# A decoder trunk in split fp32: the tiles of the split weights made 256 bytes longer, and consecutive chunks begun at eight different offsets

## The chip, the cores and the metric

The kernel runs on one core of one Trainium2 chip. The metric is device time in microseconds of one execution; lower is better. The kernel before took 2110.1 us, the median of 3 runs (2109.5 to 2110.94).

## The reference

The reference is a decoder trunk of two layers on 256 positions of width 2048, all in float32. Layer A mixes with a gated MLP over chunks of 128 positions, layer B with 12 heads of latent attention; both attend to 256 memory tokens with 4 heads, and both end in a feed-forward block of width 5632 with a causal convolution of width 3. Cut to the products that fill the time:

```python
def conv_ffn(h, w_up, cw, cb, w_down):
    a = h @ w_up                                   # 2048 x 11264
    ap = jnp.pad(a, ((0, 0), (CONV_W - 1, 0), (0, 0)))
    c = sum(ap[:, k:k + S] * cw[k] for k in range(CONV_W)) + cb
    gate, val = c[..., :D_FF], c[..., D_FF:]
    return (jax.nn.silu(gate) * val) @ w_down      # 5632 x 2048

for l in range(DEPTH):
    h = rmsnorm(x, g_mix[l])
    ...                                            # z = h @ w_in, main mixer, memory attention
    x = x + jnp.concatenate([main, mo], axis=-1) @ w_out[l]
    x = x + conv_ffn(rmsnorm(x, g_ffn[l]), w_ffn_up[l], conv_w[l], conv_b[l], w_ffn_down[l])
return rmsnorm(x, g_final)
```

## The kernel before

Every large product is computed in three matmuls of the type fp32r. Each operand is split into a high part (rounded to fp32r) and a low part (the rest): x = hi + lo, w = whi + wlo, and the product is hi whi + hi wlo + lo whi. The activations stand transposed and split in one tile (xhl, mainhl, h, memhl, qhl, chl): for each of the blocks of 128 features 512 columns, 256 of hi and 256 of lo.

**A chunk** (method `chunk`, L92 to L129) is 128 x 1024 numbers of a weight matrix, as a rule two blocks of 128 rows by 512 columns. SP issues its DMA into a tile raw (L101). ACT rounds it into whi (L121, or L126 where a gain is multiplied in, L117 for the queries' weights), DVE takes the difference raw - whi into wlo (L122, L127, L118). There are four buffers each of raw, whi and wlo, 4096 bytes per partition each.

**Two kinds of products** use a chunk:

- `gemm_fm` (from L163, with `mm_fm` from L139): the weights are the loaded operand of TensorE, in blocks of 128 x 128, the activations stream. L144 streams 512 columns (hi and lo) under whi, L148 streams the 256 columns of hi under wlo and adds them to the half of the result that belongs to lo. Chunks are taken in pairs: 32 matmuls of L144 and 32 of L148, and the order of the two turns from pair to pair.
- `gemm_tm` (with `mm_tm`, L196 to L201): the activations are loaded, the weights stream, 512 columns: L199 (hi, whi), L200 (hi, wlo), L201 (lo, whi).

Every matmul carries its own weight load. Results are evicted by ACT and DVE (`join`, L239 and L241; `split`, L246 and L247), with POOL beside them.

**The order.** Each engine's order of instructions is laid down when the program is built: a scheduler with a timeline moves instructions past each other where data and buffers allow it. How many buffers a tile has therefore enters the order. SP's queue holds the weights' DMAs in the order of the chunks; a DMA waits for DVE to have read the buffer's earlier contents.

**What else the change touches.** `conv_consts` (from L337) loads four small matrices craw by DMA (L344), transposes each on TensorE (L345) into one PSUM tile and copies that to cT; it runs once for each layer, near the end of the memory's products (90 to 101 us). Their space is given to layer A's tiles later, among them positions (L356, L358). `rope_angles` (L353 to L386) makes cos and sin, `rope_tables` (L395) transposes them. The tile u (L741 to L745) is used in layer A's gate after that. In layer B's attention `scores` (from L878) makes a head's products (L885 to L887), and ACT writes their exponentials into a tile p (L896), DVE scales it (L901); `turn` transposes p on TensorE (L908), ACT copies that to pT (L910), and `attend` multiplies (L917, L918). The loop works on the heads in pairs, some steps apart. L624 and L625, in the feed-forward block's convolution, work on a tile from its second and third element on.

The few lines that say how a chunk is used:

```python
hi = self.wp.tile([P, 1024], F32R, tag="whi", name=self.uid("whi"), bufs=4)
lo = self.wp.tile([P, 1024], F32R, tag="wlo", name=self.uid("wlo"), bufs=4)
...
nc.scalar.activation(hi[:, :n], raw[:, :n], AF.Copy)
nc.vector.tensor_tensor(lo[:, :n], raw[:, :n], hi[:, :n].bitcast(F32), ALU.subtract)
...
mm(acc[:, :], wh, x, start=first, stop=last)                  # L144
mm(acc[:, S:], wl, x[:, :S], start=False, stop=False)         # L148
```

Of the kernel before, what the change touches and what calls it, by code (L numbers as in the profile page):

```python
# [8 lines left out]
F32 = mybir.dt.float32  # L9
F32R = mybir.dt.float32r  # L10
# [6 lines left out]
P = 128  # L17
D = 2048
S = 256
# [10 lines left out]
HALF = ROPE // 2  # L30
THETA = 10000.0
EPS = 1e-6
FF_GROUPS = (4, 4, 3)


def exact_pieces(value, bits, count):
# [33 lines left out]
class Kernel:  # L70
    def __init__(self, ctx, tc, t, out):
        self.tc, self.nc, self.t, self.out = tc, tc.nc, t, out
        self.ctx = ctx
        self.n = 0
        pool = lambda name, bufs=1, **k: ctx.enter_context(tc.tile_pool(name=name, bufs=bufs, **k))
        self.cp = pool("cp")
        self.wp = pool("wp")
        self.ap = pool("ap")
        self.ps = pool("ps", 8, space=bass.MemoryType.PSUM)
# [12 lines left out]
    def chunk(self, src, nk, ncol, gains=None, twice=False, heads=None, raw=None):  # L92
        nc, n = self.nc, nk * ncol
        loaded = raw is not None
        if not loaded:
            raw = self.wp.tile([P, 1024], F32, tag="raw", name=self.uid("raw"), bufs=4)
        hi = self.wp.tile([P, 1024], F32R, tag="whi", name=self.uid("whi"), bufs=4)
        lo = self.wp.tile([P, 1024], F32R, tag="wlo", name=self.uid("wlo"), bufs=4)
        view = lambda x: x[:, :n].rearrange("p (k c) -> p k c", k=nk)
        if not loaded:  # L100
            nc.sync.dma_start(out=view(raw), in_=src)  # L101
        if twice:

            full = self.wp.tile([P, 1024], F32, tag="raw", name=self.uid("raw"), bufs=4)
            both = lambda x: x.rearrange("p (k o c) -> p k o c", o=2, c=ncol)
            src4 = raw[:, :n].rearrange("p (k o c) -> p k o c", k=nk, o=1).to_broadcast([P, nk, 2, ncol])
            g4 = gains.rearrange("p (k a b) -> p k a b", a=1, b=1).to_broadcast([P, nk, 2, ncol])
            nc.vector.tensor_tensor(both(full), src4, g4, ALU.mult)
            nc.scalar.activation(hi, full, AF.Copy)
            nc.vector.tensor_tensor(lo, full, hi.bitcast(F32), ALU.subtract)  # L110
            return tuple(x.rearrange("p (k c) -> p k c", k=nk) for x in (hi, lo))
        if heads is not None:

            s = view(raw).rearrange("p k (h c) -> p k h c", h=2)
            for c0, c1 in ((0, heads), (heads, ncol // 2)):
                o = lambda x: view(x)[:, :, 2 * c0 : 2 * c1].rearrange("p k (h c) -> p k h c", h=2)
                nc.scalar.activation(o(hi), s[:, :, :, c0:c1], AF.Copy)  # L117
                nc.vector.tensor_tensor(o(lo), s[:, :, :, c0:c1], o(hi).bitcast(F32), ALU.subtract)  # L118
            return view(hi), view(lo)
        if gains is None:  # L120
            nc.scalar.activation(hi[:, :n], raw[:, :n], AF.Copy)  # L121
            nc.vector.tensor_tensor(lo[:, :n], raw[:, :n], hi[:, :n].bitcast(F32), ALU.subtract)  # L122
        else:
            for k in range(nk):
                s = slice(k * ncol, (k + 1) * ncol)
                nc.scalar.activation(hi[:, s], raw[:, s], AF.Copy, scale=gains[k])  # L126
                nc.vector.scalar_tensor_tensor(  # L127
                    lo[:, s], raw[:, s], gains[k], hi[:, s].bitcast(F32), ALU.mult, ALU.subtract
                )  # L129
        return view(hi), view(lo)  # L130
# [206 lines left out]
    def conv_consts(self, l):  # L337
        nc, t = self.nc, self.t
        nf = 2 * FB
        acc = self.psum()  # L340
        for j in range(4):
            cr = self.tmp(self.gp, [nf, P], "craw", 4)
            src = t["conv_w"][l, j] if j < 3 else t["conv_b"][l]
            nc.sync.dma_start(out=cr, in_=src.rearrange("(k p) -> k p", p=P))  # L344
            nc.tensor.transpose(acc[:, j * nf : (j + 1) * nf], cr, self.ident[:nf, :nf])  # L345
        nc.vector.tensor_copy(self.cT[:, l], acc[:, : 4 * nf].rearrange("p (j k) -> p j k", j=4))
# [6 lines left out]
    def rope_angles(self, rt):  # L353
        nc, t = self.nc, self.t
        pi = rt.tile([2, P], I32, name="pos_i")
        nc.sync.dma_start(out=pi, in_=t["positions"].rearrange("b (a p) -> (b a) p", p=P))  # L356
        pf = rt.tile([2, P], F32, name="pos_f")
        nc.vector.tensor_copy(pf, pi)  # L358
        acc = self.psum()
        nc.tensor.transpose(acc[:, 0:2], pf, self.ident[:2, :2])  # L360
        pos = rt.tile([P, 2], F32, name="pos")
        nc.vector.tensor_copy(pos, acc[:, 0:2])
        inv = rt.tile([P, HALF], F32, name="inv")
        for i, v in enumerate(INV_FREQ):
            nc.gpsimd.memset(inv[:, i : i + 1], v)
        ang = rt.tile([P, 2, HALF], F32, name="ang")
        for a in range(2):
            nc.vector.tensor_scalar(ang[:, a, :], inv, pos[:, a : a + 1], None, ALU.mult)
        k = rt.tile([P, 2, HALF], F32, name="turns")
        magic = 12582912.0  # L370
        for scale, pieces in ((4096.0, two_pi_pieces(4096, 7, 9)), (1.0, two_pi_pieces(1, 10, 5))):
            nc.vector.tensor_scalar(k, ang, 1.0 / (2 * math.pi * scale), magic, ALU.mult, ALU.add)
            nc.vector.tensor_scalar(k, k, magic, None, ALU.subtract)
            for p in pieces:
                nc.vector.scalar_tensor_tensor(ang, k, -p, ang, ALU.mult, ALU.add)
        nc.vector.tensor_scalar(ang, ang, 3.1415925, -3.1415925, ALU.min, ALU.max)
        cos = rt.tile([P, 2, 4, HALF], F32, name="cos")
        sin = rt.tile([P, 2, 4, HALF], F32, name="sin")
        nc.scalar.activation(sin[:, :, 1, :], ang, AF.Sin)
        nc.scalar.activation(k, ang, AF.Sin, scale=0.5)  # L380
        nc.vector.tensor_tensor(k, k, k, ALU.mult)
        for j in range(4):
            nc.vector.tensor_scalar(cos[:, :, j, :], k, -2.0, 1.0, ALU.mult, ALU.add)
            if j != 1:
                nc.vector.tensor_scalar(sin[:, :, j, :], sin[:, :, 1, :], 1.0 if j == 3 else -1.0, None, ALU.mult)
        self.rope = cos, sin  # L386
# [220 lines left out]
    def ffn(self, l, after=None, to_tokens=None, tokens=None):  # L607
# [5 lines left out]
        with self.tc.tile_pool(name=self.uid("ff"), bufs=1) as fp:  # L613
            g0 = 0
            for part, ng in enumerate(FF_GROUPS):
                h = self.ap.tile([P, NB, 512], F32R, tag="big", name=self.uid("h"))
# [144 lines left out]
    def layer_b(self):  # L761
# [9 lines left out]
        with tc.tile_pool(name="lb", bufs=1) as lb:  # L771
# [73 lines left out]
            lp = ctx.enter_context(tc.tile_pool(name="lp", bufs=1))  # L845
# [32 lines left out]
            def scores(h):  # L878
                pr, j = divmod(h, 2)
                sc = self.psum()  # L880
                for qb in range(2):
                    n = P * (qb + 1)
                    o = sc[:, qb * P : qb * P + n]
                    q = slice(qb * P, (qb + 1) * P)
                    mm(o, qn[pr][:, j, q], kn[pr][:, j, :n], start=True, stop=False)  # L885
                    mm(o[:, qb * P :], self.identb, self.maskb, start=False, stop=False)
                    mm(o, qr[pr][:, q], krz[:, j, :n], start=False, stop=True)  # L887
                mx = self.tmp(lp, [P, 2], "mx", 4)
                den = self.tmp(lp, [P, 2], "den", 4)
                p = self.tmp(lp, [P, 3 * P], "p", 3)  # L890
                part = (slice(0, P), slice(P, 3 * P))
                for qb in range(2):
                    nc.vector.tensor_reduce(mx[:, qb : qb + 1], sc[:, part[qb]], AX.X, ALU.max)
                nc.vector.tensor_scalar(mx, mx, -scale, None, ALU.mult)
                for qb in range(2):
                    nc.scalar.activation(  # L896
                        p[:, part[qb]], sc[:, part[qb]], AF.Exp, bias=mx[:, qb : qb + 1], scale=scale, accum_out=den[:, qb : qb + 1]
                    )
                nc.vector.reciprocal(den, den)
                for qb in range(2):  # L900
                    nc.vector.tensor_scalar(p[:, part[qb]], p[:, part[qb]], den[:, qb : qb + 1], None, ALU.mult)  # L901
                pa[h] = p
# [30 lines left out]
            for i in range(n):  # L933
# [19 lines left out]
                if 1 <= i <= MH:  # L953
                    mscores(i - 1)
            scores(2 * n - 2)
            scores(2 * n - 1)
            for h in (2 * n - 4, 2 * n - 3):
# [95 lines left out]
```

## Time and profile before

| what | value |
|---|---|
| median of 3 runs | 2110.1 us |
| profiled execution, its own time | 2109.19 us |
| its span, first to last instruction | 2107.5 us |
| mean granted TensorE clock | 0.998 |
| HBM read, over the span | 387.88 MB, 185 GB/s |
| DMA queue of the weights, share of 16 engines | 56.7% |

The span is what the views of the profile divide; the profiled execution's own time has 1.7 us around it. PE is TensorE's matmuls, PEld its weight loads, DVE the vector engine, ACT the scalar engine, POOL GpSimd, SP the engine that issues most DMAs. A group's line names the line of the kernel, the engine, the operation, out<-in by the program's tile names, the shape, the count, then busy time and the mean in ns of one, then the idle time before. The mean of a matmul includes its passage through the array, which overlaps with the next one; the time from one matmul to the next is read from the chain of work in order of time.

### The profile page before, as it was taken

The page shows a single profiled execution, that of the slowest core. Times are in us where ns is not written, and L with a number is a line of the kernel's source. Part 1 is how long each engine was busy: PE and PEld are TensorE (multiplying, and loading weights), DVE is VectorE, ACT ScalarE, POOL GpSimd, SP SyncE. Part 2 cuts the span into 40 slices and gives each one's busy share as a digit, 9 for nine tenths or more (in the row PEclk, how much of TensorE's full clock was granted, in tenths as well). Part 3 has the DMA queues.
Part 4 walks back from the last instruction along what each step waited for, and adds up shares of the span by engine and source line. Part 5 has one row for each costly group of instructions (what it writes and reads, how often), then busy time and mean ns, then how long its engine had stood idle before and what let it go on. Part 6 is the DMA issues. An engine that isn't in the chain of part 4 may idle for free.

```text
span 2107.5 us, 30979 instructions
## 1 busy us (share of the span) xinstructions
PE 2090.7 (99%) x11600; PEld 1829.0 (87%) x11600; DVE 1460.8 (69%) x2156; ACT 1142.3 (54%) x1743; POOL 396.3 (19%) x380
## 2 busy tenths in 40 slices
PE   8999999999999999999999999999999999999998
PEld 7888888888888888888888888888888888888886
DVE  6655767777756777567798775777774677756775
ACT  7754654555535655445555564456554565535554
POOL 0100123312101211012244211321210121201220
PEclk9999999999999999999999999999999999999999
DMA  8565555655555565555555534555555656555554
GB/s 275 191 201 172 161 192 188 190 188 192 190 191 189 181 199 189 191 187 189 184 192 168 183 101 156 190 188 178 187 198 192 189 182 199 192 196 187 184 190 150
DMA packets 207852, 392.01 MB, mean 186 GB/s; under 512 B 14350, under 2 KB 23380, under 8 KB 207572
## 3 DMA queue, kind: packets, MB, share of 16 engines
q1 hardware_dynamic: 207268, 388.98, 56.7%
q8 instruction: 91, 1.49, 0.3%
q10 hardware_dynamic: 432, 1.05, 0.1%
q14 instruction: 61, 0.50, 0.1%
HBM read 387.88 MB, written 2.10 MB: 185 GB/s over the span
## 4 chain that ended last, share of the span: by engine, by line
PE 98%; DVE 1%; ACT 0%; DMA 0%; issue 0%; SPq 0%; ACTq 0%; DVEq 0%
PE ps L144 51%; PE ps L148 27%; PE ps L199 6%; PE ps L201 6%; PE ps L200 6%; PE ps L887 0%; PE ps L885 0%; PE ps L410 0%; PE ps L533 0%; PE ps L568 0%; PE ps L917 0%; DMA mtok<-in_mem 0%; PE ps L714 0%; PE ps L557 0%; PE ps L989 0%; DMA raw<-in_w_in_a 0%
## 5 line engine op out<-in xcount | busy, mean ns | idle before, releaser
L122 DVE TENSOR_TENSOR wlo<-raw,whi 128x1024 fp32r<-128x1024 f32 x660 | 842.6, 1287 | 481.7 <-ACT whi L121 358.4
L121 ACT ACTIVATE whi<-raw 128x1024 fp32r<-128x1024 f32 x660 | 698.4, 1060 | 694.9 <-PE ps L144 509.2
L144 PE MATMUL ps<-xhl,whi 128*128 128x512 f32 x3280 | 768.5, 390 | 0.0
L144 PEld LDWEIGHTS ps<-xhl,whi 128*128 128x128 f32 x3280 | 608.7, 188 | 121.6
L620 POOL TENSOR_TENSOR a<-js,rbc 128x256 f32<-128x256 f32 x176 | 231.3, 1327 | 1101.8 <-DVE js L241 1005.9
L148 PEld LDWEIGHTS ps<-xhl,wlo 128*128 128x128 f32 x3280 | 408.8, 191 | 11.1 <-DVE wlo L127 1.9
L148 PE MATMUL ps<-xhl,wlo 128*128 128x256 f32 x3280 | 413.9, 283 | 1.9 <-DVE wlo L127 1.5
L144 PE MATMUL ps<-h,whi 128*128 128x512 f32 x704 | 164.8, 390 | 0.0
L623 ACT ACTIVATE c<-a,cT 128x256 f32<-128x256 f32 x176 | 105.5, 600 | 98.2 <-POOL a L620 96.8
L144 PEld LDWEIGHTS ps<-h,whi 128*128 128x128 f32 x704 | 130.6, 188 | 26.0
L200 PE MATMUL ps<-wlo,h 128*128 128x512 f32 x352 | 136.8, 389 | 0.0
L199 PE MATMUL ps<-whi,h 128*128 128x512 f32 x352 | 136.6, 389 | 0.0
L201 PE MATMUL ps<-whi,h 128*128 128x512 f32 x352 | 136.3, 389 | 0.0
L144 PE MATMUL ps<-mainhl,whi 128*128 128x512 f32 x512 | 120.2, 390 | 0.0
L144 PEld LDWEIGHTS ps<-mainhl,whi 128*128 128x128 f32 x512 | 94.9, 188 | 18.9
L625 DVE SCALAR_TENSOR_TENSOR c<-a,cT,c 128x254 f32<-128x254 f32 x176 | 101.3, 588 | 0.0
L624 DVE SCALAR_TENSOR_TENSOR c<-a,cT,c 128x255 f32<-128x255 f32 x176 | 91.6, 540 | 12.9 <-ACT c L623 12.7
L127 DVE SCALAR_TENSOR_TENSOR wlo<-raw,gT,whi 128x512 fp32r<-128x512 f32 x112 | 87.0, 821 | 17.6 <-ACT whi L126 16.1
L126 ACT ACTIVATE whi<-raw,gT 128x512 fp32r<-128x512 f32 x112 | 74.3, 724 | 36.8 <-PE ps L144 21.4
L241 DVE TENSOR_TENSOR js<-ps,cr 128x256 f32<-128x256 f32 x209 | 82.5, 417 | 12.3 <-POOL a L620 12.3
L148 PEld LDWEIGHTS ps<-h,wlo 128*128 128x128 f32 x704 | 87.7, 191 | 2.0
L148 PE MATMUL ps<-h,wlo 128*128 128x256 f32 x704 | 88.4, 283 | 0.0
(251 smaller groups left out, 1838.9 us busy)
## 6 DMA issues: line engine op xcount, KB each, us to landing
raw<-in_w_ffn_up SPq DMA_DIRECT2D x352, 512.0 KB
raw<-in_w_ffn_down SPq DMA_DIRECT2D x176, 512.0 KB
raw<-in_w_out SPq DMA_DIRECT2D x64, 512.0 KB
raw<-in_w_in_a SPq DMA_DIRECT2D x56, 512.0 KB
raw<-in_w_mem_kv SPq DMA_DIRECT2D x31, 512.0 KB
raw<-in_w_in_b SPq DMA_DIRECT2D x16, 512.0 KB
raw<-in_w_uq SPq DMA_DIRECT2D x12, 384.0 KB
raw<-in_w_kv_a SPq DMA_DIRECT2D x8, 512.0 KB
```

The source lines that it names most:

```text
L121: nc.scalar.activation(hi[:, :n], raw[:, :n], AF.Copy)
L122: nc.vector.tensor_tensor(lo[:, :n], raw[:, :n], hi[:, :n].bitcast(F32), ALU.subtract)
L127: nc.vector.scalar_tensor_tensor(lo[:, s], raw[:, s], gains[k], hi[:, s].bitcast(F32), ALU.mult, ALU.subtract)
L144: mm(acc[:, :], wh, x, start=first, stop=last)
L148: mm(acc[:, S:], wl, x[:, :S], start=False, stop=False)
L199: mm(acc, xh, wh, start=first, stop=False)
L200: mm(acc, xh, wl, start=False, stop=False)
L201: mm(acc, xl, wh, start=False, stop=last)
L620: nc.gpsimd.tensor_tensor(a, self.join(acc), rb, ALU.mult)
L623: nc.scalar.activation(c, a, AF.Identity, scale=w(2), bias=w(3))
L624: nc.vector.scalar_tensor_tensor(c[:, 1:], a[:, : S - 1], w(1), c[:, 1:], ALU.mult, ALU.add)
L625: nc.vector.scalar_tensor_tensor(c[:, 2:], a[:, : S - 2], w(0), c[:, 2:], ALU.mult, ALU.add)
```

## The change

The tiles whi and wlo become 1088 numbers long instead of 1024 (4352 bytes instead of 4096), and a chunk uses 1024 of them from an offset of 0, 1, 2, 4, 8, 16, 32 or 64 numbers on; the offset goes around with the count of chunks. hi and lo of a chunk have the same offset. Everything that reads or writes hi and lo does so through these slices. The four buffers of each tile lie one behind the other, so a buffer now begins 256 bytes further on, against a multiple of 4096, than the one before. To make room, craw has three buffers instead of four, p two instead of three, and cos and sin take the two buffers of u.

```diff
+OFFSETS = (0, 1, 2, 4, 8, 16, 32, 64)
...
-        self.n = 0
+        self.n = self.chunks = 0
...
-        hi = self.wp.tile([P, 1024], F32R, tag="whi", name=self.uid("whi"), bufs=4)
-        lo = self.wp.tile([P, 1024], F32R, tag="wlo", name=self.uid("wlo"), bufs=4)
+
+        off = OFFSETS[self.chunks % len(OFFSETS)]
+        self.chunks += 1
+        hi, lo = (
+            self.wp.tile([P, 1088], F32R, tag=g, name=self.uid(g), bufs=4)[:, off : off + 1024] for g in ("whi", "wlo")
+        )
...
-            cr = self.tmp(self.gp, [nf, P], "craw", 4)
+            cr = self.tmp(self.gp, [nf, P], "craw", 3)
...
-        cos = rt.tile([P, 2, 4, HALF], F32, name="cos")
-        sin = rt.tile([P, 2, 4, HALF], F32, name="sin")
+        cos, sin = (self.tmp(rt, [P, S], "u", 2).rearrange("p (a j d) -> p a j d", a=2, j=4) for _ in range(2))
...
-                p = self.tmp(lp, [P, 3 * P], "p", 3)
+                p = self.tmp(lp, [P, 3 * P], "p", 2)
```

## The prediction

> **What bounds the kernel now.** I read the page first, its busy shares and its chain, then the chain in order of time in two steady stages, then the waits of TensorE, then the busy time of the engines in a steady stage.
>
> ```profile
> span 2107.5 us, 30979 instructions
> ...
> PE 2090.7 (99%) x11600; PEld 1829.0 (87%) x11600; DVE 1460.8 (69%) x2156; ACT 1142.3 (54%) x1743; POOL 396.3 (19%) x380
> ...
> PEclk9999999999999999999999999999999999999999
> ...
> PE 98%; DVE 1%; ACT 0%; DMA 0%; issue 0%; SPq 0%; ACTq 0%; DVEq 0%
> ...
> L144 PE MATMUL ps<-xhl,whi 128*128 128x512 f32 x3280 | 768.5, 390 | 0.0
> ...
> L148 PE MATMUL ps<-xhl,wlo 128*128 128x256 f32 x3280 | 413.9, 283 | 1.9 <-DVE wlo L127 1.5
> L144 PE MATMUL ps<-h,whi 128*128 128x512 f32 x704 | 164.8, 390 | 0.0
> ...
> L200 PE MATMUL ps<-wlo,h 128*128 128x512 f32 x352 | 136.8, 389 | 0.0
> ...
> L144 PE MATMUL ps<-mainhl,whi 128*128 128x512 f32 x512 | 120.2, 390 | 0.0
> ```
>
> TensorE (PE) works for 2090.7 of 2107.5 us at the full granted clock, and 98% of the chain that ended last is its own matmuls. So only two things can move the end: the time from one matmul to the next, and a wait that TensorE does not have today. The waits of TensorE, and the steady stage from 400 to 900 us (busy time of PE, weight loads, DVE, ACT, POOL):
>
> ```profile
> PE ps L333 <- DMA graw<-in_g_mem: 3.9, 1, 3.9
> PE ps L148 <- DVE wlo L127: 1.5, 2, 1.1
> PE ps L410 <- DMA mtok<-in_mem: 1.2, 2, 1.0
> ...
> 400.00:900.00 500.00, 500.00 (x2881) 442.91 (x2880) 343.41 (x483) 261.23 (x363) 77.33 (x60) 1.00 0.59 190
> ```
>
> TensorE waits for the split weights for some 2 us in the whole run. In the steady stage it is never idle, while DVE has 157 us of 500 free and ACT 239.
>
> The time from matmul to matmul comes out of the chain in order of time (start, length, what):
>
> ```profile
> 263.34 7.28 PE ps L144 x32
> 270.62 3.83 PE ps L148 x32
> 274.45 7.28 PE ps L144 x32
> 281.73 3.83 PE ps L148 x32
> ...
> 1870.00 0.23 PE ps L199
> 1870.23 0.23 PE ps L200
> 1870.45 0.23 PE ps L201
> ```
>
> A matmul of 512 columns takes 7.28 / 32 = 227.5 ns, one of 256 columns 3.83 / 32 = 119.7 ns. The difference of 107.8 ns for 256 columns makes 0.421 ns a column. Taken off the 227.5 ns, 512 x 0.421 = 215.6 ns leaves **12 ns for each matmul that are not columns**. Each of these matmuls has a weight load of its own. The lines from L199 to L201, where the split weights are the moving operand and not the loaded one, keep the same step of 0.23 us. The pairs repeat to the hundredth (7.28 and 3.83 again).
>
> The page's groups hold 3280 + 704 + 512 = 4496 matmuls of L144. L148 has one for each of them (the code issues them in pairs), and L199 to L201 have 3 x 352 = 1056. So 10,048 matmuls read whi or wlo, 8992 of them as the loaded weights. Their 12 ns add up to 121 us, the most that better addresses could give back; what they can cost has no such row.
>
> **The change, part by part.** No operation is added or removed. The order of TensorE's instructions stays, apart from transposes of the convolution's constants near 100 us; that of DVE and SP changes only there too, and ACT's and POOL's not at all.
>
> *ACT and DVE write and read split weights at odd places.* Consecutive chunks begin 0, 4, 8, 16, 32, 64, 128 and 256 bytes behind the tile's beginning. The trace has such places on DVE already: L624 writes and reads a tile from its second element on, 4 bytes off, L625 from its third; L252 is the same operation with nothing shifted.
>
> ```profile
> L624 DVE SCALAR_TENSOR_TENSOR c<-a,cT,c x176: 470/478/958, 393.5 to 2044.5; 128x255 f32<-128x255 f32 x176
> ...
> L252 DVE SCALAR_TENSOR_TENSOR xhl<-ps,gT,xhl 128x256 fp32r<-128x256 f32 x16 | 7.1, 479 | 3.1 <-ACT xhl L251 3.1
> ```
>
> The median of 478 ns for 255 elements, against a mean of 479 ns for 256, shows no cost of the 4 bytes on DVE. ACT has no such row; I bound it by nothing and by twice the time, and take nothing, after DVE's row. What hides a cost is the room in the steady stage:
>
> ```profile
> L122 DVE TENSOR_TENSOR wlo<-raw,whi 128x1024 fp32r<-128x1024 f32 x180 | 228.0, 1281 | 127.0 <-ACT whi L121 82.6 <-PE ps L148 38.4 <-issue 6.0
> ...
> L121 ACT ACTIVATE whi<-raw 128x1024 fp32r<-128x1024 f32 x181 | 191.7, 1060 | 194.6 <-PE ps L144 190.7 <-ACT h L246 3.9
> ```
>
> If the two worst offsets of eight doubled, ACT would go from 261 to 309 us of 500 and DVE from 343 to 400; both stay under TensorE. ACT also waits for TensorE to free a buffer for 190.7 us of this stage, so it runs ahead as far as four buffers let it. Term: 0.
>
> *TensorE loads weights from odd places* (8992 loads), or streams them (1056 matmuls). No row shows TensorE reading fp32r data from a tile shifted by single elements, so this is bounded from both sides. Upwards: a quarter of the chunks (4 and 8 bytes) reads slower; priced below. Downwards: the 12 ns are a collision of the load's reads with the matmul's, and another place avoids it; priced below too. The nearest row on how much room a load has is a run of four matmuls of 88 columns, each with a load of 128 columns:
>
> ```profile
> 91.60 0.47 PE L345 MATMUL ps<-ident,craw 88*128 88x88 f32 x4
> 91.85 0.47 PE L199 MATMUL ps<-whi,memhl 128*128 128x512 f32 x1
> ```
>
> Four loads and matmuls fit in 0.25 us before the next matmul starts, so a load can be had in some 63 to 80 ns, though for f32 and 88 rows. In L148 a load has 119.7 ns. So a load that takes a few columns more stays behind its matmul, and only the 12 ns that seem not to overlap could grow. If they are reading time of 128 columns, a shifted start costs at most some 4 columns more: 4/128 x 12 = 0.4 ns. On a quarter of 10,048 matmuls that is **+0.9 us**, the value I take, since the nearest rows (L624 for a shifted start, the constant 227.5 ns for the sensitivity to place) both say next to nothing.
>
> The Trainium skill has a figure for this in "SBUF — State Buffer", Specifications (TRN2): SBUF is read in lines of 16 bytes, and each cross to a new line pays a penalty. By it the 512 bytes of a load shifted by 4 or 8 bytes touch 33 lines instead of 32, 1/32 of 12 ns, which gives the same 0.9 us as an estimate; by it 16 bytes and more are free. No row here shows a line's price.
>
> *Longer tiles* move everything behind them by up to 2048 bytes, and begin every second buffer 256 bytes further on. Tiles of one kind already lie at many places (16 column blocks of 512 bytes and more) with one step of 227.5 ns. Term: 0.
>
> *Shared buffers: p.* With two buffers instead of three, ACT may write a head's p only when that of the head two before has been transposed (L908). In most of the attention that transpose stands well ahead on TensorE; not for the last pair of heads. There the written order has scores, transposes, pT:
>
> ```profile
> 1272.20 0.37 ACT L896 ACTIVATE p<-ps,mx 128x128 f32<-128x128 f32 x1 [2.07 <-DVE mx L894]
> ...
> 1273.14 0.88 ACT L910 ACTIVATE pT<-ps 128x384 f32<-128x384 f32 x2
> ...
> 1272.61 0.82 PE L908 MATMUL ps<-ident,p 128*128 128x128 f32 x6
> 1273.68 0.70 PE L917 MATMUL ps<-pT,scratch 128*128 128x256 f32 x2 [0.25 <-ACT pT L910]
> ```
>
> ACT begins that p at 1272.20 today. With two buffers it waits for the first three of the six transposes, so until about 1272.61 + 0.82 / 2, with what a semaphore takes some 1273.1. The two copies pT are queued behind it on ACT, and TensorE waits for them at L917 already (0.25 us). ACT's chain moves by 0.9 us, and TensorE with it: **+0.9 us**, once.
>
> *Shared buffers: cos, sin, craw.* cos and sin are read out before u is first written, by the order of the instructions. With three craw buffers the fourth load of each set waits on the DMA queue for a transpose:
>
> ```profile
> 92.28 1.20 SPq L344 DMA_DIRECT2D craw<-in_conv_w  x3
> 93.52 0.35 SPq L344 DMA_DIRECT2D craw<-in_conv_b  x1
> 93.97 12.42 SPq L101 DMA_DIRECT2D raw<-in_w_in_a  x6
> 107.41 0.25 SPq L356 DMA_DIRECT2D pos_i<-in_positions  x1
> ...
> 110.20 0.22 DVE L358 CAST pos_f<-pos_i 2x128 f32<-2x128 int32 x1 [0.66 <-DMA pos_i<-in_positions]
> ```
>
> The changed order puts conv_b's transpose 29 matmuls later, near 91.8 + 29 x 0.23 = 98.5 us, its load still near 92.3. The third load of the second set then waits for it behind three raw loads, near 98.6 us, and its transpose comes 25 matmuls after the first, near 104 us. A small load takes at most 2.8 us from issue to use (107.41 to 110.20), so 5 us are enough. The last transpose comes near 107 us, and the load of positions, which now waits for it, goes out at 107.4 today. Raw loads queued behind it on SP are free to go at 109.6. Term: 0; if a load is late, its like in the trace is the longest wait of 3.9 us.
>
> **Sum.** 0 (ACT, DVE) + 0.9 (TensorE's reads) + 0 (places) + 0.9 (p) + 0 (constants) = +1.8 us. The profiled execution took 2109.2 us (1.7 around its span), 0.9 under the median of 2110.1; the sum makes it 2111.0, and on the median's scale 2111.9.
>
> **Rivals.**
>
> *Slower: TensorE reads whi and wlo slower where they do not begin at a multiple of 16 bytes.* If a load took four times its 12 ns because single elements are fetched instead of groups, that is 36 ns on a quarter of 8992 loads: +81 us, 2191 on the median's scale. If streaming fell to half speed instead, 216 ns on a quarter of 1056: +57 us. Both: +138. At the least, 4 bytes alone and the 12 ns doubled: 12 x 1124 = +13 us, 2123. It decides from 1.7 ns a matmul on a quarter of them (4.2 us, 0.2%). For it: fp32r streams a column in 0.421 ns, the fastest reading in the trace, and all of it today begins at multiples of 32 bytes. Against it: DVE's L624.
>
> *Faster: the 12 ns are a collision of addresses.* By the addresses in the built program, every loaded and every streaming fp32r operand today begins at the same place modulo 512 bytes, 96. If another place frees a quarter of the matmuls: 12 x 2512 = -30 us, 2080; seven of eight: -105 us, 2005. Against it: addresses that differ by multiples of 512 bytes, and three kinds of pairs, all give 227.5 ns.
> The Trainium skill, "TensorE: Matmul & The Clock Gate", Step-by-step: what each phase is for, says that TensorE has two independent read ports and that a load takes no reading time from the running matmul. By that there is no collision and this rival is void; the 12 ns then are something else, though the same page's Wait — 56ns, not 53.3ns? gives 2.5 ns a matmul, which these rows do not show.
>
> *Slower: DVE or ACT becomes the bound.* DVE would need (500 - 343) / 228 = 69% longer splits on the average of all offsets; at twice the time for all it would be 571 us of 500, 14% longer. L624 speaks against it. A late constant (+4 us a wait) stands with it.
>
> **How the numbers follow.** Forecast (TensorE indifferent, within 0.2%, which is about what a measurement of this kernel tells from no change): 0.40, own range 2109 to 2114. TensorE slower at odd places: 0.33. DVE, ACT or a late constant: 0.06. Collisions fewer: 0.21. So faster 0.21, same 0.40, slower 0.39. The range from 2080 to 2191 reaches to the first price of each of the two large rivals; beyond lie some 0.09 on each side. The likeliest single case gives 2111.9.
>
> **What would show it.** Right: in the chain, pieces of 32 matmuls of L144 stay at 7.28 us and those of L148 at 3.83, for every chunk. Slower rival: one or two of each eight consecutive chunks have longer steps, in L144 and L148 if loading is hurt, in L199 to L201 if streaming is. Faster rival: some chunks under 227 ns. DVE rival: L122 or L121 far over 1281 and 1060 ns, and TensorE waiting for wlo. p: some 0.9 us more of TensorE waiting at L917's place near 1274 us. Constants: a wait of TensorE at L345's place between 98 and 108 us. What would make me wrong is a price of fp32r reading that no row here bears on.

## The result, and the profile after

The changed kernel takes 2126.14 us, the median of 4 runs (2126.04 to 2126.58), against 2109.91 for the kernel before in the same session: 1.0075 times, with a 95% interval of 1.0063 to 1.0087. It is 16.2 us slower. The forecast was 2111.9 with an own range of 2109 to 2114, no difference that can be measured.

The page of the kernel after, with the rows of the groups that the prediction quoted (busy us, mean ns of one, idle time before them):

```profile
span 2124.9 us, 30983 instructions
...
PE 2107.8 (99%) x11600; PEld 1822.1 (86%) x11600; DVE 1463.5 (69%) x2156; ACT 1142.6 (54%) x1743; POOL 395.4 (19%) x380
...
PEclk9999999999999999999999999999999999999999
...
PE 98%; DVE 1%; ACT 0%; DMA 0%; issue 0%; SPq 0%; DVEq 0%; ACTq 0%
...
L149 PE MATMUL ps<-xhl,whi 128*128 128x512 f32 x3280 | 781.3, 394 | 0.0
...
L153 PE MATMUL ps<-xhl,wlo 128*128 128x256 f32 x3280 | 407.5, 281 | 1.9 <-DVE wlo L132 1.5
L149 PE MATMUL ps<-h,whi 128*128 128x512 f32 x704 | 167.3, 393 | 0.0
...
L205 PE MATMUL ps<-wlo,h 128*128 128x512 f32 x352 | 138.4, 394 | 0.0
...
L149 PE MATMUL ps<-mainhl,whi 128*128 128x512 f32 x512 | 122.2, 394 | 0.0
```

L149 and L153 are L144 and L148 of the kernel before, L204 to L206 are its L199 to L201. The profiled execution took 2126.58 us, 1.7 more than its span, as before. The span grew by 17.4 us and TensorE's busy time by 17.1, at the same clock: the loss is inside the matmuls, and not in waits. The mean of one matmul is longer than its step, because matmuls are pipelined, but a step that grows by 4 ns shows as 4 ns more in the mean.

The groups say where the 17.1 us come from. The 512-column matmuls under whi became longer: 781.3 - 768.5 = 12.8, 167.3 - 164.8 = 2.5 and 122.2 - 120.2 = 2.0 us. The 256-column ones under wlo became **shorter**: 407.5 - 413.9 = -6.4 us on xhl, and less on the rest. Those that stream the weights became longer again (L205 138.4 - 136.8 = 1.6 us, and its like). The chain in order of time in a steady stage, first of the kernel after (start, length, what):

```profile
456.81 7.37 PE ps L149 x32
464.18 3.78 PE ps L153 x32
467.96 7.43 PE ps L149 x32
475.38 3.74 PE ps L153 x32
479.13 7.37 PE ps L149 x32
```

A chunk gives 8 matmuls of each kind, a pair of chunks 16, and because the order turns from pair to pair, two pairs stand in each stretch of 32, four of the eight offsets. Before, all stretches were 7.28 and 3.83. Now 7.43 / 32 = 232 ns and 3.74 / 32 = 117 ns stand where 227.5 and 119.7 stood. The time from each matmul's start to the next one's, from the trace's records, grouped by the chunk's offset (256 bytes put together with 0; the mean over all, transitions included, steps of 300 ns and more left out because they hold a wait; ns):

| offset of the chunk, bytes | 0, 256 | 4 | 8 | 16 | 32 | 64 | 128 |
|---|---|---|---|---|---|---|---|
| L149, 512 columns | 228.8 | 232.6 | 230.3 | 233.0 | 233.5 | 232.5 | 232.7 |
| L153, 256 columns | 120.2 | 118.0 | 116.8 | 119.0 | 117.5 | 114.6 | 119.8 |

The kernel before has 227.7 and 120.0. No offset but 0 leaves the long matmuls alone, and the offsets that are multiples of 16 bytes are no better than 4 and 8.

The waits of TensorE, and its steady stage from 400 to 900 us, in the kernel after:

```profile
PE ps L338 <- DMA graw<-in_g_mem: 2.9, 1, 2.9
PE ps L414 <- DMA mtok<-in_mem: 1.9, 2, 1.7
PE ps L153 <- DVE wlo L132: 1.5, 2, 1.1
PE ps L921 <- ACT pT L914: 1.1, 1, 1.1
...
400.00:900.00 500.00, 500.00 (x2863) 437.75 (x2862) 344.28 (x484) 262.77 (x366) 79.36 (x62) 1.00 0.62 189
```

Nobody makes TensorE wait in the stage; it gets through 2863 matmuls there instead of 2881.

### The profile page after: what moved, and what is told of

Its sections match the earlier page's. It is cut to its first block, busy times and chain, and to the rows that moved or that the text cites. A ratio compares the mean times of both kernels' runs of the same rounds, so it can differ in the third digit from the quotient of the medians.

```text
span 2124.9 us, 30983 instructions
## 1 busy us (share of the span) xinstructions
PE 2107.8 (99%) x11600; PEld 1822.1 (86%) x11600; DVE 1463.5 (69%) x2156; ACT 1142.6 (54%) x1743; POOL 395.4 (19%) x380
## 4 chain that ended last, share of the span: by engine, by line
PE 98%; DVE 1%; ACT 0%; DMA 0%; issue 0%; SPq 0%; DVEq 0%; ACTq 0%
PE ps L149 52%; PE ps L153 26%; PE ps L206 6%; PE ps L205 6%; PE ps L204 6%; PE ps L891 0%; PE ps L889 0%; PE ps L414 0%; PE ps L537 0%; PE ps L572 0%; PE ps L921 0%; PE ps L718 0%; DMA mtok<-in_mem 0%; PE ps L912 0%; DMA raw<-in_w_in_a 0%; PE ps L561 0%
## 5 line engine op out<-in xcount | busy, mean ns | idle before, releaser
L126 ACT ACTIVATE whi<-raw 128x1024 fp32r<-128x1024 f32 x660 | 698.9, 1060 | 711.0 <-PE ps L149 516.3
L149 PE MATMUL ps<-xhl,whi 128*128 128x512 f32 x3280 | 781.3, 394 | 0.0
L149 PEld LDWEIGHTS ps<-xhl,whi 128*128 128x128 f32 x3280 | 608.8, 188 | 133.1
L624 POOL TENSOR_TENSOR a<-js,rbc 128x256 f32<-128x256 f32 x176 | 230.3, 1321 | 1112.5 <-DVE js L246 1016.5
L153 PEld LDWEIGHTS ps<-xhl,wlo 128*128 128x128 f32 x3280 | 402.7, 189 | 12.0 <-DVE wlo L132 1.9
L153 PE MATMUL ps<-xhl,wlo 128*128 128x256 f32 x3280 | 407.5, 281 | 1.9 <-DVE wlo L132 1.5
L149 PE MATMUL ps<-h,whi 128*128 128x512 f32 x704 | 167.3, 393 | 0.0
L149 PEld LDWEIGHTS ps<-h,whi 128*128 128x128 f32 x704 | 130.6, 188 | 28.3
L205 PE MATMUL ps<-wlo,h 128*128 128x512 f32 x352 | 138.4, 394 | 0.0
L204 PE MATMUL ps<-whi,h 128*128 128x512 f32 x352 | 138.1, 393 | 0.0
L206 PE MATMUL ps<-whi,h 128*128 128x512 f32 x352 | 138.1, 394 | 0.0
L149 PE MATMUL ps<-mainhl,whi 128*128 128x512 f32 x512 | 122.2, 394 | 0.0
L149 PEld LDWEIGHTS ps<-mainhl,whi 128*128 128x128 f32 x512 | 94.9, 188 | 20.7
L153 PEld LDWEIGHTS ps<-h,wlo 128*128 128x128 f32 x704 | 86.3, 188 | 2.2
L153 PE MATMUL ps<-h,wlo 128*128 128x256 f32 x704 | 86.8, 280 | 0.0
```

The source lines that it names most:

```text
L204: mm(acc, xh, wh, start=first, stop=False)
L205: mm(acc, xh, wl, start=False, stop=False)
L206: mm(acc, xl, wh, start=False, stop=last)
L624: nc.gpsimd.tensor_tensor(a, self.join(acc), rb, ALU.mult)
```

## The experiments

In what follows a **step** is the time from the start of one matmul to the start of the next of the same product, a **place** is the address of a tile modulo 256 bytes, and a place is given as the distance of the loaded operand's first byte from the streamed one's. Where a mean step has decimals it is a mean over the start times in the trace's records, without the first 12 of a stretch and without steps that hold a wait, or a stretch's length in the chain over its 32 matmuls. A mean over all steps, transitions included, is called so.

**All offsets 0** (longer tiles and shared buffers stay):

```diff
-OFFSETS = (0, 1, 2, 4, 8, 16, 32, 64)
+OFFSETS = (0,)
```

> The longer tiles and the shared buffers alone, every chunk at offset 0. All three theories (the step depends on where the loaded weights lie against the stream modulo 256 bytes; only starts off a multiple of 16 bytes cost; only the change of offset from chunk to chunk costs) expect the time of before plus the 0.9 us of the p buffers: 2110.8 us, steps of 227 and 120 ns in L149 and L153. A time near 2126 would put the loss on the shared buffers or the longer tiles.

Measured: 2110.89 us, 1.0005 times (0.9995 to 1.0014). In the chain the stretches are those of the kernel before:

```profile
464.31 7.28 PE ps L149 x32
471.59 3.83 PE ps L153 x32
475.42 7.28 PE ps L149 x32
```

So the offsets make the loss, and what stands beside them costs under 1 us. The buffers here begin 256 bytes further on from one to the next, and the steps do not notice: a shift by 256 bytes counts as none.

**All offsets 16 numbers, 64 bytes:**

```diff
-OFFSETS = (0, 1, 2, 4, 8, 16, 32, 64)
+OFFSETS = (16,)
```

> Every chunk at the one offset of 16 numbers (64 bytes). Place against the stream: L153 settles at 113 to 114 ns (4744 x -6 = -28 us), L149 at some 232 (4744 x +5 = +24), so 2100 to 2115 us, with steps that differ from those of before. Odd starts alone: 2110.8 and the steps of before, since 64 bytes is a multiple of 16. Change from chunk to chunk alone: the same 2110.8, since nothing changes from chunk to chunk.

Measured: 2111.85 us, 1.0009 times (1.0000 to 1.0019). That looks like nothing, but the chain says otherwise:

```profile
464.74 7.46 PE ps L149 x32
472.20 3.63 PE ps L153 x32
475.83 7.46 PE ps L149 x32
483.29 3.63 PE ps L153 x32
```

A matmul of 512 columns takes 7.46 / 32 = 233.1 ns, 5.6 more than before, one of 256 columns 3.63 / 32 = 113.4, 6.3 less. Gain and loss cancel within 2 us. 64 bytes are a multiple of 16, and all chunks begin alike, so two explanations fall here as the whole cause: odd starts, and the change from one chunk to the next.

**A scan: one offset for each product,** 0 to 240 bytes in steps of 16, and 0 to 60 bytes in steps of 4 (`gemm_tm` counts in the same way):

```diff
-        off = OFFSETS[self.chunks % len(OFFSETS)]
+        off = OFFSETS[self.products % len(OFFSETS)]
...
     def gemm_fm(...):
+        self.products += 1
```

> One offset for a whole product, in steps of 16 bytes from 0 to 240, the next product the next. Place against the stream: each product has a steady step of its own, L153 between 113 and 124 ns and L149 between 226 and 236, lowest in L153 near 64 bytes. Odd starts alone: 227 and 120 in all of them, 2111 us. Change alone: 227 and 120 from the second pair of chunks of each product on.

> The same with offsets of 0, 4, 8 to 60 bytes, one for a product. Place against the stream: steady steps that move smoothly or in steps with the offset, those at 16, 32 and 48 bytes as in the scan by 16 bytes. Odd starts alone: 227 and 120 at 0, 16, 32 and 48 bytes and longer steps at the twelve others. Change alone: 227 and 120 everywhere past the first pair of a product.

Measured: 2130.0 and 2132.27 us, one run each. The mean steps at ten of the places, in ns:

| place, bytes | 0 | 8 | 16 | 28 | 32 | 52 | 64 | 128 | 208 | 240 |
|---|---|---|---|---|---|---|---|---|---|---|
| whi loaded, 512 columns | 226.8 | 230.5 | 227.7 | 229.6 | 233.2 | 233.4 | 233.3 | 233.3 | 231.7 | 228.0 |
| wlo loaded, 256 columns | 120.0 | 115.6 | 118.3 | 116.6 | 118.3 | 113.3 | 115.7 | 118.7 | 116.7 | 118.0 |

Three things stand in it. Place 0, where the kernel before has everything, is the best of all for 512 columns and one of the worst for 256. Places that are no multiple of 16 bytes are no worse than those that are. And many of the values are mixtures. (Where both scans have a place, the value is that of the scan with steps of 16 for 0, 16, 32 and 64 bytes; at 16 bytes the other one has 233.2 and 118.5, so under whi the two scans, which were expected to agree there, do not.) The column at 64 bytes mixes stretches with steps of 113 and others with 117 and 118, in one product whose whi and wlo all lie at 64 (L148 and L152 are L144 and L148 of the kernel before):

```profile
464.03 3.77 PE ps L152 x32
467.80 7.46 PE ps L148 x32
475.26 3.64 PE ps L152 x32
```

The run with everything at 64 bytes shows the same on a small scale: 124 of its 128 longer stretches under wlo settle at 113 to 114 ns, the other four at 118. So the place does not settle the step alone: at these places TensorE falls into one of two step lengths and mostly keeps it for a whole stretch.

**wlo alone at 64 bytes, and whi alone at 64 bytes,** by gaps ahead of and behind the four buffers, in the kernel before:

```diff
+    def gap(self, name, n):
+        if name not in self.gaps:
+            self.gaps.add(name)
+            self.nc.vector.memset(self.wp.tile([P, n], F32, name=name), 0.0)
...
+        self.gap("gap0", 16)
         lo = self.wp.tile([P, 1024], F32R, tag="wlo", name=self.uid("wlo"), bufs=4)
+        self.gap("gap1", 48)
```

(in the second run the two gaps stand around hi instead)

> The kernel before (its longer buffers untouched) with 64 bytes of gap ahead of the four wlo tiles and 192 behind them, so that wlo alone lies 64 bytes on from the streamed operand, modulo 256, and whi lies at 0 as before. Theory (the step hangs on the loaded operand's place against the streamed one's, modulo 256 bytes, each pair for itself): the 256-column steps of L153's counterpart fall from 120 to 114 ns as with everything at 64, 4,624 times 6 ns = 28 us; the 512-column steps of whi stay at 227; where wlo is streamed (448 matmuls of the time-major product) some 2 ns each are lost, 1 us. About 2083 us, 0.987. Rival 1 (what counts is that whi and wlo lie alike, so that one load follows the other at the same place): the 512-column steps get longer too, 2100 or more. Rival 2 (TensorE gains, but then waits for the split weights of VectorE and ScalarE): the steps fall to 114, the waits for wlo and whi rise by as much, 2105 to 2110.

> The counterpart: whi alone 64 bytes on, wlo at 0, buffers as before. Theory (place against the stream modulo 256 bytes, each pair for itself): the 512-column steps that load whi rise from 227 to 233 ns, 4,624 times 5.5 = 25 us, the 256-column steps stay at 120, and in the time-major product 896 matmuls that stream whi lose 2 ns, 2 us: about 2137 us, 1.013. Rival (whi and wlo must lie alike): the time of the run with wlo alone at 64 bytes, and both kinds of step change.

Measured: 2108.39 us, 0.9993 times (0.9984 to 1.0002), and 2144.25 us, 1.0162 times (1.0148 to 1.0176). Two rows from the groups of each, first wlo alone, then whi alone (L152 and L156 are L144 and L148, L208 is L200):

```profile
L152 PE MATMUL ps<-xhl,whi 128*128 128x512 f32 x3280 | 768.3, 390 | 0.0
L156 PE MATMUL ps<-xhl,wlo 128*128 128x256 f32 x3280 | 407.6, 281 | 2.0 <-DVE wlo L135 1.6 <-DVE wlo L130 0.4
...
L208 PE MATMUL ps<-wlo,h 128*128 128x512 f32 x352 | 138.4, 394 | 0.0
```

```profile
L152 PE MATMUL ps<-xhl,whi 128*128 128x512 f32 x3280 | 787.6, 396 | 0.0
L156 PE MATMUL ps<-xhl,wlo 128*128 128x256 f32 x3280 | 412.3, 283 | 1.7 <-DVE wlo L135 1.3 <-DVE wlo L130 0.4
```

With whi alone moved, its matmuls grow from 390 to 396 ns and wlo's stay at 283, as expected; the time is 7 us above the 2137 expected, mostly because the time-major product loses 9.8 us in place of 2 (its mean over all steps went from 226.9 to 233.1 ns). With wlo alone moved, whi's stay at 390, but wlo's fall by 2 ns only and not by 6, and in the time-major product all three matmuls grew to 394, also those that stream the unmoved whi; gain and loss cancel. TensorE's waits are as before, so it doesn't wait for another engine. My theory, each pair of places for itself, is half refuted: the place counts, but with wlo at 64 bytes the steps are 113.4 ns in nearly all stretches when whi lies there too, and 117.8 in all of them (3.77 us for 32) when whi lies at 0.

Another engine could lengthen the steps without a wait, since ACT and DVE read and write the same tiles. The traces speak against it: settled steps during which ACT, DVE and POOL were all idle are as long as those during which ACT and DVE both worked. Under whi that is 226.7 against 226.7 ns in the kernel before and 233.3 against 233.5 with whi alone at 64 bytes; under wlo alone at 64 bytes it is 118.2 against 117.7 (93 to 95 idle steps under whi, 89 under wlo).

**wlo alone at 52 bytes,** where the scan had its best, only in the products of `gemm_fm`, which load it (wlo's buffers stay 1088 numbers long, whi's are back at 1024, the other shared buffers stay; 88 of the 4744 matmuls that load wlo come from elsewhere and stay at 0):

```diff
-        hi, lo = (
-            self.wp.tile([P, 1088], F32R, tag=g, name=self.uid(g), bufs=4)[:, off : off + 1024] for g in ("whi", "wlo")
-        )
+        hi = self.wp.tile([P, 1024], F32R, tag="whi", name=self.uid("whi"), bufs=4)
+        lo = self.wp.tile([P, 1088], F32R, tag="wlo", name=self.uid("wlo"), bufs=4)[:, place : place + 1024]
...
-                hi, lo = self.chunk(src(kbs[c], nk), nk, nblk * P, g, raw=raw if c == 0 else None)
+                hi, lo = self.chunk(src(kbs[c], nk), nk, nblk * P, g, raw=raw if c == 0 else None, place=13)
```

> The changed kernel's shared buffers, whi at 0 always, wlo 52 bytes (13 numbers) on from the tile's beginning in the products that load it, 0 where it is streamed. Theory (place against the stream modulo 256 bytes): the 256-column steps fall from 120 to 113.3 ns, the lowest of the scan by 4 bytes, 4,496 times 6.7 ns = 30 us; nothing is lost in the time-major product; the shared buffers cost 0.8 us as with all places at 0. About 2081 us, 0.986. Rival 1 (a start that is not a multiple of 16 bytes costs something): above the run with wlo at 64 bytes by over 5 us. Rival 2 (TensorE then waits for VectorE or ScalarE): 2105 to 2110.

Measured: 2108.44 us, 0.9994 times (0.9985 to 1.0003), and not the 2081 expected. The steps of wlo go 120, 118, 122 and again, 120 in the mean, and not 113.3, and TensorE waits 1.5 us for wlo as before, so the gain is missing and not hidden behind a wait. What differs from the scan is that there whi lay at 52 bytes too.

**Everything 64 bytes on alike,** the streamed operands too:

```diff
         self.cp = pool("cp")
+        self.nc.vector.memset(self.cp.tile([P, 16], F32, name="shift"), 0.0)
```

> The kernel before with a 64-byte tile ahead of all others, so that raw, whi, wlo and every streamed operand lie 64 bytes on alike. Theory (place against the stream): steps of 227 and 120 ns as before, 2110 us, 1.000 within 0.001. Rival (the place of the loaded operand alone counts): steps of 233 and 114 ns as with only the weights at 64 bytes; the sum is then about the same, 2112, so the steps tell, not the time.

Measured: 2109.99 us, 1.0000 times (0.9991 to 1.0009), and the two main groups of before to the digit, with stretches of 7.28 and 3.83 us in the chain:

```profile
L145 PE MATMUL ps<-xhl,whi 128*128 128x512 f32 x3280 | 768.5, 390 | 0.0
L149 PE MATMUL ps<-xhl,wlo 128*128 128x256 f32 x3280 | 413.9, 283 | 1.9 <-DVE wlo L128 1.5 <-DVE wlo L123 0.4
```

It is where the operands lie against each other, and not where one of them lies.

**wlo's place scanned alone,** 4 bytes further for each product of `gemm_fm`, whi at 0 (the edit is against the run at 52 bytes; `gemm_fm` counts the products as in the scans):

```diff
-..., place=13)
+..., place=self.products % 64)
```

> As the run with wlo at 52 bytes, but another place of wlo for each feature-major product, 0 to 252 bytes in steps of 4, whi always at 0. Theory now (the matmuls fall into a repeated pattern of steps, and which one is set by the places and by the pattern that TensorE comes from): the 256-column steps have steady means between 113 and 122 ns, at 0 bytes 120, at 64 bytes 118 (as with wlo alone at 64) and not the 114 of the run with all at 64, at 52 bytes 120 and not the 113.3 of the scan in which whi was moved too; the 512-column steps settle at 226.7 whatever wlo's place. Time 2102 to 2112. Rival (the place of the pair that is at work alone): 114 at 64 and 113.3 at 52, and the same table as in the scans that moved whi as well.

Measured: 2106.75 us, one run; whi's steps 226.7 ns throughout. The chain in the products with wlo at 52, at 64 and at 76 bytes:

```profile
417.11 3.84 PE ps L148 x32
420.95 7.26 PE ps L144 x32
...
483.63 3.77 PE ps L148 x32
487.40 7.28 PE ps L144 x32
...
549.98 3.64 PE ps L148 x32
553.62 7.28 PE ps L144 x32
```

3.84 at 52 bytes and 3.77 at 64 are what the two runs with wlo alone moved gave (120.0 and 117.8 ns a step) and not what the scan by 4 bytes (113.3 at 52) and the run with all at 64 bytes (113.4) gave, in which whi was moved too. The place of wlo works together with that of whi, whose matmuls alternate with wlo's. Of the 64 places, 76, 88 and 180 bytes stand out, with 113.8 to 114.0 ns over all steps of the one product each of them had; six places from 192 to 212 had 8 matmuls each and tell nothing.

**Another order, all places as before:** each matmul under whi stands beside the one under wlo of the same block, in `mm_fm`:

```diff
+        for j in jobs:
+            for f in (low, high) if j[5] else (high, low):
+                f([j])
```

> The kernel before, all places as before, but each 512-column matmul with whi stands beside the 256-column one with wlo of the same block, instead of all of one kind and then all of the other. Theory (a pattern of steps set by places and by what runs before): the pair doesn't take 226.7 + 120 = 346.7 ns; it settles on another value some 6.7 ns or more away, 340 or 353 or above, which moves the time by 30 us or more either way, 2080 or 2140. Rival (each kind of step has its own length, whatever stands beside it): 346.7 a pair, fewer transitions, 2105 to 2110.

Measured: 2130.06 us, one run, 20.8 us more than the kernel before in that session:

```profile
L144 PE MATMUL ps<-xhl,whi 128*128 128x512 f32 x3280 | 1145.6, 399 | 0.0
L148 PE MATMUL ps<-xhl,wlo 128*128 128x256 f32 x3280 | 884.9, 281 | 0.0
```

Here the means count, not the busy sums, which overlap. No address differs from the kernel before, yet 512 columns take 9 ns more and 256 columns 2 less. In a long stretch the steps repeat after three pairs: 241, 120, 236, 113, 232, 118 ns, which is 1060 / 3 = 353 ns a pair instead of 346.7. The order alone moves the steps. The time is 10 us under the 2140 expected for 353: over all steps, transitions included, the pair went from 347.7 to 352.5, since the kernel before has transitions too. One thing goes with the order: four matmuls in a row, not two, add into the same tile of ps. The steps repeat every three pairs and that tile changes every two, so they don't follow it, but no run separates the two.

**wlo at 76 and at 88 bytes** in all products of `gemm_fm` (against the run at 52 bytes):

```diff
-..., place=13)
+..., place=19)
```

(and `place=22`)

> wlo 76 bytes on in all feature-major products, whi at 0, the changed kernel's shared buffers. Theory (repeated patterns, set by the places and by the pattern that TensorE comes from): in the scan with whi at 0 one product of 64 such steps had a mean of 113.8 ns at 76 bytes; if all products come from the same pattern of whi, 4,600 steps lose 6.5 ns each, 30 us, and with 0.8 us for the shared buffers the time is 2081 us, 0.986. If most products enter in another phase, the steps lie at 117 to 118 ns and the time at 2098 to 2102. Rival (the mean over products is 120 whatever the place, the scan's 113.8 being one product's luck): 2108 or more.

> The same at 88 bytes, where the scan's one product had 114.0 ns: by the theory 2082 us, 0.987, if all products come from the same pattern of whi, 2098 to 2102 if most enter in another phase; by the rival 2108 or more.

Measured: 2085.39 us, 0.9883 times (0.9868 to 0.9897), and 2086.9 us, 0.9890 (0.9873 to 0.9906). Both beat the kernel before, by 24.5 and 23.0 us. The chain and the group at 76 bytes:

```profile
455.80 3.64 PE ps L148 x32
459.44 7.28 PE ps L144 x32
466.72 3.64 PE ps L148 x32
470.36 7.28 PE ps L144 x32
```

```profile
L144 PE MATMUL ps<-xhl,whi 128*128 128x512 f32 x3280 | 770.0, 391 | 0.0
...
L148 PE MATMUL ps<-xhl,wlo 128*128 128x256 f32 x3280 | 395.1, 277 | 2.1 <-DVE wlo L127 1.6
```

wlo's matmuls on xhl give back 413.9 - 395.1 = 18.8 us, and those on h and mainhl 7 more; whi's keep their 7.28. The time is 4 us above the 2081 that I gave. The first three steps of a stretch are 117, 118 and 119 ns before it settles at 113, 113, 114, so the mean over all steps is higher: 114.4 ns, 5.6 less than the 120.0 of the kernel before and not 6.5. And whi's matmuls on xhl take 1.5 us more here (at 88 bytes they do not).

## Where the prediction was right and where it was wrong

The measured 2126.14 us lies between 2080 and 2191, but that range had been drawn to hold both large rivals; the forecast itself, a TensorE that is indifferent to the places, did not come true. The 16 us are also a remainder: some 25 us of longer steps less some 8 us of shorter ones.

- **The bound** was right. TensorE's steps set the end, before and after; no wait of TensorE grew by more than 0.8 us.
- **ACT and DVE at odd places, 0:** right. In the view of tile wlo the median of DVE's full chunks is 1226 ns after and 1225 before, and in that of whi ACT's is 1062 after and 1063 before, here the two rows of the kernel after:

```profile
L127 DVE TENSOR_TENSOR wlo<-raw,whi x660: 1207/1226/1769, 99.8 to 2106.0; 128x1024 fp32r<-128x1024 f32 x165
```

```profile
L126 ACT ACTIVATE whi<-raw x660: 1039/1062/1101, 98.7 to 2104.9; 128x1024 fp32r<-128x1024 f32 x165
```

- **TensorE's reads, +0.9 us: this step failed.** It measured some +16 us, by the steps between starts: +18 on the 512-column matmuls under whi, -8 on the 256-column ones under wlo, +7 where the weights stream. The step priced a longer read of loads that begin 4 or 8 bytes off, at 4/128 of 12 ns, on a quarter of the matmuls. What the runs showed in its place is an effect of the operands' places on the steps of all matmuls, at 16, 32 and 64 bytes as well as at 4 and 8, with both signs. (The count was short too: with the smaller groups that the page leaves out, 11,096 matmuls read whi or wlo and not 10,048, which would have made the term 1.0.)
- **Why I took it so low:** "the constant 227.5 ns for the sensitivity to place". This was the real mistake. The places that the trace of before shows are all one place: column blocks 512 bytes apart, tiles that begin at 96 modulo 512 (in the built program that holds for both operands of all 11,096 matmuls). A constant over them says nothing of 64 bytes. I had written the fact down under the faster rival, and then counted it against that rival ("addresses that differ by multiples of 512 bytes, and three kinds of pairs, all give 227.5 ns"), though it bears on neither side.
- **Longer tiles, 0:** right as far as it goes; with all offsets 0 the steps are those of before.
- **p, +0.9 us:** right in size and place. The wait for pT went from 0.3 to 1.1 us, +0.8, about what the run with all offsets 0 lost in all, and ACT's write of p now waits for the transpose (the timeline of the kernel after):

```profile
1280.18 0.82 PE L912 MATMUL ps<-ident,p 128*128 128x128 f32 x6
...
1280.71 0.37 ACT L900 ACTIVATE p<-ps,mx 128x128 f32<-128x128 f32 x1 [3.00 <-PE ps L912]
...
1282.06 0.70 PE L921 MATMUL ps<-pT,scratch 128*128 128x256 f32 x2 [1.06 <-ACT pT L914]
```

- **Constants, 0:** right. TensorE has no wait at the transposes of craw.
- **The slower rival** had the sign and, at its lower end of 2123, nearly the size, but not the mechanism, so that nearness is luck. Six of eight offsets lengthen the steps under whi, where it expected one or two; multiples of 16 bytes are not free: 64 bytes on whi alone cost 34 us. The rule of the Trainium skill on lines of 16 bytes ("SBUF — State Buffer", Specifications (TRN2)) gives no difference between 0 and 64 bytes; the chains of these two runs differ by 5.6 and 6.3 ns a step, so it is not what decides here.
- **The faster rival** had the right kind of cause, operands' addresses modulo a power of two, and a wrong direction for this change. Place 0 is already the best of those scanned for 512 columns, so the other places could only lose there. But its promise for the 256-column steps was real: one better place for wlo alone gives 24.5 us. That this is near the 30 that I had priced is chance: the price was 12 ns on a quarter of the matmuls, the gain is 5.6 ns on those under wlo.
- **The page that spoke against a collision** (the Trainium skill, "TensorE: Matmul & The Clock Gate", Step-by-step: what each phase is for: two independent read ports, so that a load takes no reading time from the running matmul) cannot be used as a rule for the time of these fp32r matmuls: moving only whi, by 64 bytes, takes the step from 227 to 233 ns. Whether it is the two reads that collide, no run shows. On the strength of it and of the constant step I gave collisions 0.21.

**What is shown and what is not.** Shown: the steps depend on the relative places of the operands modulo 256 bytes (all moved alike, nothing changes; 256 bytes, nothing changes; one moved, its steps change); on what TensorE did before (wlo at 64 bytes gives 113.4 ns in nearly all stretches with whi at 64 and 117.8 with whi at 0, and, with all places equal, some stretches settle at 113.3 and others at 117.8); and on the order of the matmuls (same places, 353 or 346.7 ns a pair). Of the settled stretches of all runs but the one with another order, almost nine in ten under whi have a mean near 226.7 or 233.3 ns, and seven in ten under wlo one near 113.3 or 120.0, which are 34, 35, 17 and 18 times 6.67; most others under wlo lie between 117.5 and 118.5. My reading, that the load of the next weights and the stream of the running matmul take turns at some shared resource, that TensorE falls into a repeated pattern, and that a pattern loses one, two or three turns of 6.67 ns a matmul, fits these means, but it is argued. Which resource it is, why 76 bytes is good and 52 is not when whi lies at 0, and what makes a stretch take one of two patterns at equal places, stays open: no run separates the load's reads from its writing into the array.

## What to carry to other kernels

A constant in a trace is evidence only over what varied: list the values that the quantity took (here addresses modulo 256 bytes, of which there was one) before calling a cost insensitive. Where TensorE is never idle, look at its steps by operand pair and by order, since a few ns a matmul over some 11,000 of them were 24 us less and 34 us more here; and a place found in a scan has to be tried with the rest of the kernel's places as they will be. A change that mixes a gain and a loss, as the run with all at 64 bytes did (5.6 ns up, 6.3 down, 1.0009 times in all), should be read by groups, not by its time.

## What the runs showed of the hardware that I had not expected

- fp32r matmuls of 128 x 128 weights with 512 columns take 226.7 ns a step at the best place seen, up to 234.3 in the settled stretches under whi, and up to 238 in the mean of a place where the weights stream; with 256 columns 113.3 to 122.7.
- The cost beyond the columns is not a constant 12 ns, as the prediction had it. By the difference of 226.7 and 120.0, a column takes 0.417 ns; beyond that the steps show 13.3 ns (226.7 and 120.0), 6.7 (113.3) or 20 (233.3).
- The pattern is persistent: after a change from one operand to the other it takes some three to five steps to settle (233, 236, 228, 233, 231 and then 227, 227, 226 for whi in the kernel before), and as a rule it then repeats over the whole stretch.
